# The meta tokens' products of 16 rows and 512 columns as two of 256 columns, from rows 0 and 32

## The chip, the cores and the metric

One core of a Trainium2 chip runs one program. The metric is the device time of one execution in microseconds (us). Names used throughout: PE is TensorE's matmuls, PEld its weight loads, DVE VectorE, ACT ScalarE, POOL GpSimd, SP the queue that issues the weight transfers, and PSUM the matmuls' output memory with banks of 512 float32 columns.

## The reference

Two blocks of a language model over 272 tokens: 16 learned meta tokens ahead of 256 real ones. The change is in the second block, which has two layers of this form (cut to what matters):

```
u = rmsnorm(h); proj = u @ w_in
pool_out = silu(pool_g) * pool_mixer(pool_v)
ssd_out  = ssd_mixer(...)        # chunks: 16 meta tokens, 128, 128
attn_out = silu(a_g) * attention # 8 heads, 2 kv heads, the same chunks as keys
h = h + rmsnorm(concat(pool_out, ssd_out, attn_out) @ w_out)

# ssd, per chunk and group of 8 heads
states = einsum('bcsgn,bcgrs,bcsgrp->bcgrpn', bm, decay_states, x * dt)
# attention, per kv head with its 4 query heads
o = einsum('bqgrk,bqkgd->bqgrd', softmax(logits), v)
```

The sum over the keys (k) and over a chunk's tokens (s) is the contraction of a matmul, so the meta tokens' part of it contracts over 16 rows only. Between the layers h has all 272 tokens; the second layer's output drops the meta tokens, so there the meta tokens serve only as keys and as the first state.

## The kernel before, in words

Activations lie with channels on the 128 partitions and tokens in columns. Nearly all of the work is `unit`: a projection's block of 128 output channels is summed over 16 (or 8) slices of 128 input channels, three matmuls a slice (`pj<-xh,whi`, `pj<-xl,whi`, `pj<-xh,wlo`), after ACT and DVE have split each 128x1024 piece of weights into a high (`whi`) and a low part (`wlo`). These are matmuls of type float32r over 256 to 272 columns.

What the heads need beside that runs as separate streams (Python generators) whose instructions are merged into the row of `pj` matmuls; their PSUM tiles are called `mx` (four buffers, `pst()`), and their matmuls are plain float32, which the trace shows as two passes each; a transpose (`tp`, L295, against the identity `c`) is one pass. A scheduler with a timing model of its own places every engine's instructions; each engine then runs its row strictly in order.

Three streams of the second block make the meta products. `attention` turns the values v around once per layer (`vT`, one tile for each of the three chunks of keys). `back_attention` handles each query chunk `ci` and kv head: probabilities `pr`, four transposes a key chunk into one PSUM tile, a copy to `pT`, then `po += vT.T @ pT` over the key chunks, 512 columns being 4 heads by 128 queries. `back_ssd` handles each group g of 8 heads: per chunk four transposes of x (`cx`) into `xd` and, times the decay, `xw`; one transpose of bm into `bt`; then the state `st = bt.T @ xw`, 128 by 512. In both, the meta chunk's product has operands of 16 rows. `back_dt` makes the transposed tables (`tdt`, `tdl`) with the decays per layer.

Of the kernel before, what the change touches and what calls it, by code (L numbers as in the profile page):

```python
# [17 lines left out]
P = 128  # L18
NM = 16
# [219 lines left out]
class Kernel:  # L239
# [53 lines left out]
    def tp(self, out, in_):  # L293
        n = in_.shape[0]
        return self.PE.transpose(out, in_, self.cst("ident")[:n, :n])  # L295

    def split(self, hi, lo, x):
        self.act(hi, x)
# [1250 lines left out]
    def back_dt(self, x):  # L1549
        reg, l, nc = self.early, self.l, self.nc  # L1550
        sm = lambda *shape, name, rows=P: self.p2.tile([rows, *shape], F32, tag="d_" + name, name=name, bufs=1)

        yield 6.0
        dt, cs, dl = (reg(T, rows=32, name=i) for i in ("dt", "cs", "dl"))
        base, tot = (reg(2, 8, rows=32, name=i) for i in ("base", "tot"))
        lp = self.log1pexp(x, 32, T, reg)
        self.stt(dt, x, 0.0, ALU.max, lp, ALU.add)
        da = x
        self.ts(da, dt, self.a, ALU.mult, -1.0, ALU.mult)
        self.V.tensor_tensor_scan(out=cs, data0=self.cst("sscan")[:32], data1=da, initial=0.0, op0=ALU.mult,  # L1560
                                  op1=ALU.add)
        cb = cs[:, NM:].rearrange("p (c b t) -> p c b t", c=2, b=8)
        self.V.tensor_copy(tot, cb[:, :, :, 15])
        self.V.memset(base[:, :, 0:1], 0.0)
        for c in range(2):
            self.V.tensor_tensor_scan(out=base[:, c, 1:], data0=self.cst("ones")[:32, :7], data1=tot[:, c, :7],
                                      initial=0.0, op0=ALU.mult, op1=ALU.add)
        for c in range(2):
            self.add(cb[:, c], cb[:, c], base[:, c].unsqueeze(2).to_broadcast([32, 8, 16]))
        self.dbg(f"L{l}cs", cs)  # L1570
        self.csd = self.dr.tile([32, T], F32, name=f"csd{l}")
        nc.gpsimd.dma_start(self.csd, cs)
        for o, m in ((0, NM), (NM, P)):
            self.ts(dl[:, o:o + m], cs[:, o:o + m], -1.0, ALU.mult, cs[:, o + m - 1:o + m], ALU.add)
        self.act(dl[:, :NM + P], dl[:, :NM + P], AF.Exp)

        self.tcs, self.tdt, self.tdl, self.tec = (sm(3, 32, name=f"t{i}") for i in range(4))
        yield 5.0
        pt = self.pst()
        p4 = pt[:, :288].rearrange("p (c x h) -> p c x h", c=3, x=3)  # L1580
        chunks = ((0, NM), (NM, P), (NM + P, P))
        for c, (o, m) in enumerate(chunks):
            for x_, src in enumerate((cs, dt, dl)):
                if c < 2 or x_ < 2:
                    self.tp(p4[:m, c, x_], src[:, o:o + m])
        for c, (o, m) in enumerate(chunks):
            self.act(self.tcs[:m, c], p4[:m, c, 0])
            self.act(self.tdt[:m, c], p4[:m, c, 1])
            self.act(self.tec[:m, c], p4[:m, c, 0], AF.Exp)
            if c < 2:  # L1590
                self.act(self.tdl[:m, c], p4[:m, c, 2])
        yield 1.0

    def rope(self, tmp, x, kind, o, n):
# [16 lines left out]
    def attention(self):  # L1611
        reg, l, o0, n = self.reg, self.l, self.o0, self.n
        all_ = slice(0, T)
        fl = lambda t: t.rearrange("p a b -> p (a b)")
        chunks = ((0, NM), (NM, P), (NM + P, P))
        qi = []
        for j in range(4):
            q = reg(2, n, name="qi")
            yield from self.unit(f"L{l}i_q{j}", self.xs, self.outc, lambda i, ps: self.nrm(q[:, i], ps, self.outc))
            self.rope(self.rt[j % 2][:, :, :n], q, "i", o0, n)  # L1620

            qs = [self.early(2, n, name="qs").bitcast(F32R) for _ in range(2)]
            for hh in range(2):
                r, o = slice(64 * hh, 64 * hh + 64), slice(64 - 64 * hh, 128 - 64 * hh)
                self.act(qs[hh][r], q[r])
                self.sub(qs[hh][o], q[r], qs[hh][r].bitcast(F32))
            qi.append(qs)
            if j == 0:

                self.tiw = self.p2.tile([P, 3, 32], F32, tag="d_tiw", name="tiw", bufs=1)  # L1630
                pt = self.pst()
                p3 = pt[:, :96].rearrange("p (c h) -> p c h", c=3)
                for c, (o, m) in enumerate(chunks):
                    if o + m > self.o0:
# [12 lines left out]
        qs, gs = [], []  # L1647
        for j in range(4):
            q = reg(2, n, name="q")
            yield from self.unit(f"L{l}a_q{j}", self.xs, self.outc, lambda i, ps: self.nrm(q[:, i], ps, self.outc))  # L1650
            self.rope(self.rt[j % 2][:, :, :n], q, "q", o0, n)
            qs.append(q)
            yield 1.0
            if j == 0:
                vT = []
                for o, m in chunks:
                    pt = self.pst()
                    for j in range(2):
                        self.tp(pt[:m, P * j:P * j + P], v[:, j, o:o + m])
# [48 lines left out]
    def back_attention(self, ng, k, vT, qs, gs):  # L1708
        reg, l, o0 = self.reg, self.l, self.o0
        chunks = ((0, NM), (NM, P), (NM + P, P))  # L1710
        sc = 128 ** -0.5
        for ci, (o, m) in enumerate(chunks):
# [3 lines left out]
            for kv in range(2):  # L1716
# [16 lines left out]
                pT = []  # L1733
                for si, (so, sn) in keys:
                    yield 1.0
                    pt = self.pst()
                    for i in range(4):
                        self.tp(pt[:sn, m * i:m * i + m], pr[i // 2][:, i % 2, so:so + sn])
                    t = reg(4 * m, rows=sn, name="pT")
# [6 lines left out]
                po = self.pst()  # L1746
                for x, (si, _) in enumerate(keys):
                    self.mm(po[:, :4 * m], vT[si][:, kv], pT[x], start=x == 0, stop=x == len(keys) - 1)
                for i in range(2):
                    self.stt(self.mix[:, 24 + 4 * kv + 2 * i:26 + 4 * kv + 2 * i, o - o0:o - o0 + m],  # L1750
                             po[:, 2 * m * i:2 * m * i + 2 * m].rearrange("p (h t) -> p h t", h=2), 0.5, ALU.mult,
                             gs[2 * kv + i][:, :, o - o0:o - o0 + m], ALU.mult)

    def front_ssd(self, g):
# [25 lines left out]
    def back_ssd(self, g, bc, xs, zs):  # L1780
# [20 lines left out]
        xd, st = [], []  # L1801
        for c, (o, m) in enumerate(chunks):
            yield 1.0
            pt = self.pst()
# [4 lines left out]
            xd.append(t)  # L1809
            if c == 2:  # L1810
                break
            w = reg(512, rows=m, name="xw")
# [7 lines left out]
            pS = self.pst()  # L1820
            self.mm(pS, bt, w)
            s = reg(512, name="st")
            if c == 0:
                self.act(s, pS)
            else:
                ed = self.p2.tile([P, 8], F32, tag="ed", name="ed", bufs=2)
                nc.gpsimd.dma_start(ed, self.csd[hs, NM + P - 1:NM + P].rearrange("(o h) t -> o (h t)", o=1)
                                    .to_broadcast([P, 8]))
                self.act(ed, ed, AF.Exp)
                self.mul(h8(s, P), h8(st[0], P), ed.unsqueeze(2).to_broadcast([P, 8, 64]))  # L1830
                self.add(s, s, pS)
            st.append(s)
        Ls = None
        y = [reg(2, n, name="y") for _ in range(2)]
# [114 lines left out]
```

## Time and profile before

| | before |
|---|---|
| time, median of 3 runs | 2941.95 us (2938.15 to 2943.53) |
| profiled execution | 2941.08 us |
| its span, first to last instruction | 2939.3 us |
| PE busy | 2890.7 us, 98% |
| DVE / ACT / POOL busy | 68% / 49% / 6% |
| mean granted TensorE clock | 0.994 |

A busy share is the time in which an engine had at least one instruction in flight. A matmul's duration in the trace overlaps the next one's, so what a matmul costs is read from the distance between starts, not from its duration.

### The profile page before, as it was taken

What the parts mean: (1) busy time and instruction counts of PE and PEld (TensorE: products, weight loads), DVE (VectorE), ACT (ScalarE), POOL (GpSimd) and SP (SyncE); (2) the same over time, 40 slices, a digit from 0 to 9 for tenths busy, and PEclk for the clock granted to TensorE, in tenths of its full rate; (3) what the DMA queues carried; (4) which work ended last, traced back from release to release, by engine and by line L of the source; (5) the groups of instructions that cost most, each with busy time, mean ns of one, the idle gap of its engine ahead of it and who ended that gap; (6) DMA issues with size and microseconds to landing.
All of it is one profiled execution on the core that took longest, in us unless ns stands there. A gap on an engine that the chain in (4) does not pass through costs nothing.

```text
span 2939.3 us, 56854 instructions
## 1 busy us (share of the span) xinstructions
PE 2890.7 (98%) x23398; PEld 2790.3 (95%) x23398; DVE 2003.0 (68%) x3520; ACT 1429.4 (49%) x2051; POOL 169.8 (6%) x331
## 2 busy tenths in 40 slices
PE   8999999999999999999999999999989999999997
PEld 8999999989999999999999999999989999999997
DVE  7657668657565555668866877764579678887555
ACT  6445546445354444456434444444465444444453
POOL 1101001001000000002000010000021000000000
PEclk9999999999999999999999999999999999999999
DMA  6534435435446565666554455555555545556553
GB/s 225 161 113 136 145 103 148 129 117 163 136 134 187 186 186 184 185 199 211 162 180 144 136 164 161 174 179 173 177 167 162 188 143 154 184 172 187 175 185 122
DMA packets 135028, 480.42 MB, mean 163 GB/s; under 512 B 18056, under 2 KB 18576, under 8 KB 134768
## 3 DMA queue, kind: packets, MB, share of 16 engines
q1 hardware_dynamic: 122112, 441.80, 48.0%
q0 software_dynamic: 12224, 33.90, 4.3%
q8 instruction: 183, 3.00, 0.4%
q10 hardware_dynamic: 432, 1.09, 0.1%
q14 instruction: 77, 0.63, 0.1%
HBM read 468.40 MB, written 7.02 MB: 162 GB/s over the span
## 4 chain that ended last, share of the span: by engine, by line
PE 94%; DVE 3%; DMA 1%; ACT 1%; issue 1%; POOL 0%; DVEq 0%; ACTq 0%; POOLq 0%
PE pj L291 81%; PE mx L291 11%; PE mx L295 2%; DVE wlo L270 1%; DMA wraw<-in_w_dram 1%; ACT L267 0%; DVE out L270 0%; DVE h L270 0%; DMA LB<-ld 0%; ACT whi L267 0%; DVE xl L288 0%; DMA h<-in_xt_dram 0%; POOL db L270 0%; DMA ld<-Dc 0%; DVE yc L270 0%
## 5 line engine op out<-in xcount | busy, mean ns | idle before, releaser
L291 PE MATMUL pj<-xh,whi 128*128 128x272 f32 (+2 forms) x6080 | 1749.5, 288 | 17.6 <-ACT xh L267 14.8
L291 PE MATMUL pj<-xh,wlo 128*128 128x272 f32 (+2 forms) x6080 | 1745.0, 287 | 1.0 <-DVE wlo L270 1.0
L291 PE MATMUL pj<-xl,whi 128*128 128x272 f32 (+2 forms) x6080 | 1744.1, 287 | 1.0 <-DVE xl L288 1.0
L267 ACT ACTIVATE whi<-wraw 128x1024 fp32r<-128x1024 f32 x840 | 886.9, 1058 | 1204.3 <-PE pj L291 1021.8
L270 DVE TENSOR_TENSOR wlo<-wraw,whi 128x1024 fp32r<-128x1024 f32 x840 | 1024.4, 1221 | 572.4 <-ACT whi L267 569.9
L291 PEld LDWEIGHTS pj<-xh,whi 128*128 128x128 f32 x6080 | 1142.2, 188 | 34.1 <-ACT xh L267 15.2
L291 PEld LDWEIGHTS pj<-xh,wlo 128*128 128x128 f32 x6080 | 1147.0, 189 | 10.7 <-issue 6.1
L291 PEld LDWEIGHTS pj<-xl,whi 128*128 128x128 f32 x6080 | 1145.4, 188 | 9.9 <-issue 5.1
L291 PE MATMUL pj<-yh,whi 128*128 128x256 f32 x384 | 108.1, 282 | 0.0
L291 PE MATMUL pj<-yl,whi 128*128 128x256 f32 x384 | 108.0, 281 | 0.0
L291 PE MATMUL pj<-yh,wlo 128*128 128x256 f32 x384 | 107.8, 281 | 0.0
L267 ACT ACT_TABLE_LOAD x79 | 101.4, 1283 | 4.3 <-PEq L1938 1.7
L291 PE MATMUL pj<-ml,whi 128*128 128x256 f32 x256 | 73.2, 286 | 0.0
L291 PE MATMUL pj<-mh,whi 128*128 128x256 f32 x256 | 73.2, 286 | 0.0
L291 PE MATMUL pj<-mh,wlo 128*128 128x256 f32 x256 | 72.9, 285 | 0.0
L291 PEld LDWEIGHTS pj<-yh,wlo 128*128 128x128 f32 x384 | 72.4, 189 | 0.0
L291 PEld LDWEIGHTS pj<-yh,whi 128*128 128x128 f32 x384 | 72.4, 189 | 0.0
L291 PEld LDWEIGHTS pj<-yl,whi 128*128 128x128 f32 x384 | 72.3, 188 | 0.0
L288 DVE SCALAR_TENSOR_TENSOR cx<-ct,hcw,cx 128x271 f32<-128x271 f32 (+2 forms) x144 | 64.3, 493 | 0.0
L291 PEld LDWEIGHTS pj<-mh,whi 128*128 128x128 f32 x256 | 49.6, 194 | 0.0
L291 PEld LDWEIGHTS pj<-mh,wlo 128*128 128x128 f32 x256 | 49.5, 193 | 0.0
L291 PEld LDWEIGHTS pj<-ml,whi 128*128 128x128 f32 x256 | 49.5, 193 | 0.0
(493 smaller groups left out, 2576.2 us busy)
## 6 DMA issues: line engine op xcount, KB each, us to landing
wraw<-in_w_dram SPq DMA_DIRECT2D x838, 512.0 KB, 3.5
L<-csd POOLq DMA_DIRECT2D x32, 256.0 KB, 4.9
LB<-ld POOLq DMA_DIRECT2D x12, 480.0 KB, 8.8
h<-in_xt_dram POOLq DMA_DIRECT2D x8, 272.0 KB, 9.5
h<-hd POOLq DMA_DIRECT2D x8, 272.0 KB, 3.8
hd<-h POOLq DMA_DIRECT2D x8, 272.0 KB, 2.4
res<-in_xt_dram POOLq DMA_DIRECT2D x8, 256.0 KB, 4.4
hd<-acc POOLq DMA_DIRECT2D x8, 256.0 KB, 3.6
```

Source lines behind the costliest of these rows:

```text
L267: return self.S.activation(out, in_, func, **kw)
L270: return (eng or self.V).tensor_tensor(out=out, in0=a, in1=b, op=op)
L288: return self.V.scalar_tensor_tensor(out=out, in0=a, scalar=s, in1=b, op0=op0, op1=op1)
L291: return self.PE.matmul(out, lhsT, rhs, start=start, stop=stop)
L295: return self.PE.transpose(out, in_, self.cst("ident")[:n, :n])
```

## The change

The meta chunk's operands come to lie twice below each other: heads' first half on rows 0 to 15, second half on rows 32 to 47 of a 64-row tile. The product of 16 rows by 512 columns becomes two of 16 rows by 256 columns, one from rows 0, one from rows 32, each into a PSUM bank of its own. To bring data to rows 32 and up, the new helper `tp32` transposes 32 columns instead of 16 (16 meta tokens and the 16 after them, which are not used) for row 0, and does the same with a plain matmul against the identity for row 32.

```
+    def tp32(self, out, row, cols, in_):
+        n, o = in_.shape[0], out[row:row + 32, cols]
+        if row == 0:
+            return self.tp(o, in_)
+        return self.mm(o, in_, self.cst("ident")[:n, :n])
...
@@ back_dt
+        self.mul(wm[:, :32], dt[:, :32], dl[:, :32])
+        for x in range(2):
+            self.tp32(pt, 32 * x, slice(0, 32), wm[:, :32])
+        self.act(self.twm, pt[:64, :32])
...
@@ attention (vT of the meta chunk)
+                            for x in range(2):
+                                self.tp32(pt, 32 * x, slice(P * j, P * j + P), v[:, j, :32])
...
@@ back_attention
+                    if si == 0 and ci:
+                        for i in range(4):
+                            self.tp32(pt, 32 * (i // 2), slice(m * (i % 2), m * (i % 2) + m), pr[i // 2][:, i % 2, :32])
+                        t = reg(2 * m, rows=64, name="pT")
+                        self.V.tensor_copy(t, pt[:64, :2 * m])
...
-                for x, (si, _) in enumerate(keys):
-                    self.mm(po[:, :4 * m], vT[si][:, kv], pT[x], start=x == 0, stop=x == len(keys) - 1)
+                    pos = [self.pst()[:, :2 * m] for _ in range(2)]
+                    for x in range(1, len(keys)):
+                        for i in range(2):
+                            self.mm(pos[i], vT[x][:, kv], pT[x][:, 2 * m * i:2 * m * i + 2 * m], start=x == 1, stop=False)
+                    for i in range(2):
+                        r = slice(32 * i, 32 * i + NM)
+                        self.mm(pos[i], vT[0][r, kv], pT[0][r], start=False, stop=True)
...
@@ back_ssd (meta chunk)
+                for i in range(4):
+                    self.tp32(pt, 32 * (i // 2), slice(P * (i % 2), P * (i % 2) + P), xs[i // 2][:, i % 2, :32])
+                for x in range(2):
+                    r = slice(32 * x, 32 * x + NM)
+                    self.mul(h4(w[r]), h4(pt[r, :256]),
+                             self.twm[r, 8 * g + 4 * x:8 * g + 4 * x + 4].unsqueeze(2).to_broadcast([NM, 4, 64]))
+                for x in range(2):
+                    self.tp32(pt, 32 * x, slice(0, P), bc[:, 0, :32])
+                self.act(bt, pt[:64, :P])
+                pS = [self.pst() for _ in range(2)]
+                for x in range(2):
+                    r = slice(32 * x, 32 * x + NM)
+                    self.mm(pS[x][:, :256], bt[r], w[r])
+                for x in range(2):
+                    self.act(s[:, 256 * x:256 * x + 256], pS[x][:, :256])
+                if o < o0:
+                    xd.append(None)
+                    continue
```

The four transposes of 16 columns for `xd` stay in the first layer, where the meta tokens have outputs, and fall away in the second. The key chunks of 128 rows keep their columns, in two matmuls of 256 instead of one of 512. In the whole program 12 matmuls of 128 rows by 512 columns become 24 by 256, 16 of 16 rows by 512 become 32 by 256 (16 from rows 32), 76 transposes of 16 columns become 16 (those of `xd`) plus 44 of 32 columns, and 44 plain matmuls of 32 columns are new, besides one transpose and one matmul of 32 by 32 in each layer.

The scheduler places the new instructions. First PE's row in the first layer's attention, chunk 1, kv head 0 (`pr` are the probabilities, `c_66` the identity; L295 is a transpose, L291 a plain matmul; the size is the output's). Before:

```order
L291 MATMUL pj<-xl,whi 128x272
L295 MATMUL mx<-c_66,pr 16x128
L295 MATMUL mx<-c_66,pr 128x128
L295 MATMUL mx<-c_66,pr 16x128
L295 MATMUL mx<-c_66,pr 128x128
L295 MATMUL mx<-c_66,pr 16x128
L295 MATMUL mx<-c_66,pr 128x128
L295 MATMUL mx<-c_66,pr 16x128
L295 MATMUL mx<-c_66,pr 128x128
L291 MATMUL pj<-xh,wlo 128x272
```

And with the change:

```order
L291 MATMUL pj<-xl,whi 128x272
L295 MATMUL mx<-c_66,pr 32x128
L295 MATMUL mx<-c_66,pr 128x128
L295 MATMUL mx<-c_66,pr 32x128
L295 MATMUL mx<-c_66,pr 128x128
L291 MATMUL mx<-c_66,pr 32x128
L295 MATMUL mx<-c_66,pr 128x128
L291 MATMUL mx<-c_66,pr 32x128
L295 MATMUL mx<-c_66,pr 128x128
L291 MATMUL pj<-xh,wlo 128x272
```

The two plain matmuls to rows 32 stand singly between transposes of 128 columns.

Second, PE's row in the first layer's SSD, group 1, where x (`cx`) and bm (`cx` too) of the meta chunk are turned around. Before, the four transposes of x:

```order
L291 MATMUL pj<-xl,whi 128x272
L291 MATMUL pj<-xh,wlo 128x272
L295 MATMUL mx<-c_66,cx 16x128 x4
L291 MATMUL pj<-xh,whi 128x272
L291 MATMUL pj<-xl,whi 128x272
```

With the change, x and bm follow each other:

```order
L291 MATMUL pj<-xh,whi 128x272
L291 MATMUL mx<-z,c_66 128x272
L295 MATMUL mx<-c_66,cx 32x128 x2
L291 MATMUL mx<-c_66,cx 32x128 x2
L295 MATMUL mx<-c_66,cx 32x128
L291 MATMUL mx<-c_66,cx 32x128
L291 MATMUL pj<-xl,whi 128x272
```

Two of x's transposes became plain matmuls, and bm's one transpose became a transpose and a plain matmul.

Third, the same group's state product (`xw,bt`). Before:

```order
L291 MATMUL pj<-xl,whi 128x272
L291 MATMUL pj<-xh,wlo 128x272
L291 MATMUL pj<-xh,whi 128x272
L291 MATMUL mx<-xw,bt 128x512
L295 MATMUL mx<-c_66,cx 128x128 x4
L291 MATMUL pj<-xl,whi 128x272
```

With the change:

```order
L291 MATMUL pj<-xh,whi 128x272
L291 MATMUL mx<-xw,bt 128x256
L291 MATMUL pj<-xl,whi 128x272
L291 MATMUL pj<-xh,wlo 128x272
L291 MATMUL pj<-xh,whi 128x272
L291 MATMUL pj<-xl,whi 128x272
L291 MATMUL mx<-xw,bt 128x256
L295 MATMUL mx<-c_66,cx 16x128 x4
L295 MATMUL mx<-c_66,cx 128x128 x4
```

The two halves are four `pj` matmuls apart. So are they in groups 2 and 3 of the first layer (seven apart) and group 0 of the second (one apart); the other four pairs of the SSD, and all eight of the attention, stand next to each other.

## Rows read from the trace of the kernel before

**Rows 1.** The page: busy us, share of the span, instructions of each engine.
```profile
PE 2890.7 (98%) x23398; PEld 2790.3 (95%) x23398; DVE 2003.0 (68%) x3520; ACT 1429.4 (49%) x2051; POOL 169.8 (6%) x331
```

**Rows 2.** The page: chain that ended last, share of the span by engine.
```profile
PE 94%; DVE 3%; DMA 1%; ACT 1%; issue 1%; POOL 0%; DVEq 0%; ACTq 0%; POOLq 0%
```

**Rows 3.** Waits of PE, 1370 to 2939: us in total, times, longest; first and last.
```profile
PE pj L291 <- ACT xh L267: 6.2, 1, 6.2
...
PE pj L291 <- DVE v L270: 0.8, 1, 0.8
```

**Rows 4.** Waits of DVE, same stretch: the longest in total.
```profile
DVE wlo L270 <- ACT whi L267: 285.9, 270, 3.2
```

**Rows 5.** Groups by form, PE, same stretch: the two meta products, by passes.
```profile
L291 PE MATMUL mx<-xw,bt 16*128 16x512 f32 x16 | 9.0, 640 | 0.0
...
L291 PE MATMUL mx<-pT,vT 16*128 16x512 f32 x16 | 8.9, 633 | 0.0
```

**Rows 6.** Timeline of PE at a meta product: start us, us, instruction, passes.
```profile
1614.34 0.29 PE L291 MATMUL pj<-xh,wlo 128*128 128x272 f32 x1
1614.47 0.29 PE L291 MATMUL pj<-xh,whi 128*128 128x272 f32 x1
1614.68 1.12 PE L291 MATMUL mx<-xw,bt 16*128 16x512 f32 x2
1615.73 0.73 PE L291 MATMUL mx<-k,q 128*128 128x272 f32 x2
1616.30 0.60 PE L295 MATMUL mx<-c,cx 128*128 128x128 f32 x4
1616.65 0.37 PE L291 MATMUL pj<-xl,whi 128*128 128x272 f32 x1
```

**Rows 7.** Timeline of PE at a state product of 128 rows.
```profile
1627.49 1.02 PE L291 MATMUL mx<-xw,bt 128*128 128x512 f32 x2
1628.35 0.60 PE L295 MATMUL mx<-c,pr 128*128 128x128 f32 x4
```

**Rows 8.** Timeline, first block: four matmuls of 64 rows, from rows 0 and 64.
```profile
37.68 0.28 PE L291 MATMUL pj<-xh,wlo 128*128 128x258 f32 x1
37.89 1.19 PE L291 MATMUL mx<-wa,wup 64*128 64x272 f32 x8
39.01 0.39 PE L291 MATMUL pj<-xh,whi 128*128 128x258 f32 x1
```

**Rows 9.** Timeline, first block: one matmul of 16 rows, 256 columns.
```profile
605.99 0.69 PE L291 MATMUL mx<-Dm,vm 16*128 16x256 f32 x2
606.62 0.92 PE L291 MATMUL mx<-D,vT 128*128 128x256 f32 x4
```

**Rows 10.** Timeline: four transposes of 16 columns among full matmuls.
```profile
1607.00 0.60 PE L295 MATMUL mx<-c,cx 128*16 128x128 f32 x4
1607.43 0.62 PE L291 MATMUL mx<-k,q 128*128 128x272 f32 x2
```

**Rows 11.** Timeline, first block: plain matmuls of 32 output columns.
```profile
307.33 0.29 PE L291 MATMUL pj<-xh,whi 128*128 128x272 f32 x1
307.55 0.44 PE L291 MATMUL mx<-E 128*32 128x32 f32 x8
307.91 0.40 PE L291 MATMUL pj<-xl,whi 128*128 128x272 f32 x1
308.14 0.29 PE L291 MATMUL pj<-xh,wlo 128*128 128x272 f32 x1
```

**Rows 12.** Timeline, first block: plain matmuls of 64 output columns.
```profile
167.73 0.65 PE L291 MATMUL mx<-Rk,vT 128*64 128x128 f32 x4
168.31 0.39 PE L291 MATMUL pj<-xh,whi 128*128 128x272 f32 x1
```

**Rows 13.** Timeline: four transposes right behind a meta product.
```profile
1700.45 0.65 PE L295 MATMUL mx<-c,cx 128*128 128x128 f32 x4
1700.86 0.37 PE L291 MATMUL pj<-xl,whi 128*128 128x272 f32 x1
```

More of the change, by code (lines that the diff above doesn't have):

```diff
@@ L1577, in back_dt @@
         self.tcs, self.tdt, self.tdl, self.tec = (sm(3, 32, name=f"t{i}") for i in range(4))
+        self.twm = sm(32, rows=64, name="twm")
+        wm = reg(32, rows=32, name="wm")
         yield 5.0
         pt = self.pst()
+        self.mul(wm[:, :32], dt[:, :32], dl[:, :32])
         p4 = pt[:, :288].rearrange("p (c x h) -> p c x h", c=3, x=3)
@@ L1591, in back_dt @@
                 self.act(self.tdl[:m, c], p4[:m, c, 2])
+        pt = self.pst()
+        for x in range(2):
+            self.tp32(pt, 32 * x, slice(0, 32), wm[:, :32])
+        self.act(self.twm, pt[:64, :32])
         yield 1.0
@@ L1657, in attention @@
                     pt = self.pst()
+                    m = m if o else 64
                     for j in range(2):
-                        self.tp(pt[:m, P * j:P * j + P], v[:, j, o:o + m])
+                        if o:
+                            self.tp(pt[:m, P * j:P * j + P], v[:, j, o:o + m])
+                        else:
+                            for x in range(2):
+                                self.tp32(pt, 32 * x, slice(P * j, P * j + P), v[:, j, :32])
                     t = reg(2, P, rows=m, name="vT")
@@ L1736, in back_attention @@
                     pt = self.pst()
+                    if si == 0 and ci:
[3 more added lines that the diff above has]
+                        self.V.tensor_copy(t, pt[:64, :2 * m])
+                        pT.append(t)
+                        continue
                     for i in range(4):
@@ L1745, in back_attention @@
                 yield 1.0
-                po = self.pst()
-                for x, (si, _) in enumerate(keys):
-                    self.mm(po[:, :4 * m], vT[si][:, kv], pT[x], start=x == 0, stop=x == len(keys) - 1)
+                if ci == 0:
+                    po = self.pst()
+                    self.mm(po[:, :4 * m], vT[0][:m, kv], pT[0])
+                    pos = [po[:, :2 * m], po[:, 2 * m:4 * m]]
+                else:
+                    pos = [self.pst()[:, :2 * m] for _ in range(2)]
[5 more added lines that the diff above has]
+                        self.mm(pos[i], vT[0][r, kv], pT[0][r], start=False, stop=True)
                 for i in range(2):
                     self.stt(self.mix[:, 24 + 4 * kv + 2 * i:26 + 4 * kv + 2 * i, o - o0:o - o0 + m],
-                             po[:, 2 * m * i:2 * m * i + 2 * m].rearrange("p (h t) -> p h t", h=2), 0.5, ALU.mult,
+                             pos[i].rearrange("p (h t) -> p h t", h=2), 0.5, ALU.mult,
                              gs[2 * kv + i][:, :, o - o0:o - o0 + m], ALU.mult)
@@ L1803, in back_ssd @@
             yield 1.0
+            if c == 0:
+                pt = self.pst()
+                for i in range(4):
+                    self.tp32(pt, 32 * (i // 2), slice(P * (i % 2), P * (i % 2) + P), xs[i // 2][:, i % 2, :32])
+                w = reg(256, rows=64, name="xw")
+                h4 = lambda t: t.rearrange("p (h v) -> p h v", h=4)
+                for x in range(2):
+                    r = slice(32 * x, 32 * x + NM)
+                    self.mul(h4(w[r]), h4(pt[r, :256]),
+                             self.twm[r, 8 * g + 4 * x:8 * g + 4 * x + 4].unsqueeze(2).to_broadcast([NM, 4, 64]))
+                yield 1.0
+                pt = self.pst()
+                for x in range(2):
+                    self.tp32(pt, 32 * x, slice(0, P), bc[:, 0, :32])
+                bt = reg(P, rows=64, name="bt")
+                self.act(bt, pt[:64, :P])
+                yield 1.0
+                pS = [self.pst() for _ in range(2)]
+                for x in range(2):
+                    r = slice(32 * x, 32 * x + NM)
+                    self.mm(pS[x][:, :256], bt[r], w[r])
+                s = reg(512, name="st")
+                for x in range(2):
+                    self.act(s[:, 256 * x:256 * x + 256], pS[x][:, :256])
+                st.append(s)
+                if o < o0:
+                    xd.append(None)
+                    continue
+                yield 1.0
             pt = self.pst()
@@ L1809, in back_ssd @@
             xd.append(t)
+            if c == 0:
+                continue
             if c == 2:
@@ L1822, in back_ssd @@
             s = reg(512, name="st")
[L1823 to L1831, printed above, removed]
+            ed = self.p2.tile([P, 8], F32, tag="ed", name="ed", bufs=2)
+            nc.gpsimd.dma_start(ed, self.csd[hs, NM + P - 1:NM + P].rearrange("(o h) t -> o (h t)", o=1)
+                                .to_broadcast([P, 8]))
+            self.act(ed, ed, AF.Exp)
+            self.mul(h8(s, P), h8(st[0], P), ed.unsqueeze(2).to_broadcast([P, 8, 64]))
+            self.add(s, s, pS)
             st.append(s)
```

## The prediction

> **What bounds the kernel now.** I read the page first: PE has something in flight for 98% of the span [rows 1], and the chain that ended last runs over PE for 94% [rows 2]. Busy is a weak measure, since matmuls overlap, so I went on to who waits for whom. In the stretch in which the second block runs (1370 to 2939 us) PE waits in six rows, from 6.2 down to 0.8 us, 12.4 us together [rows 3], and by the timeline these lie where one layer ends and the next begins. DVE on the other hand waits 285.9 us there for ACT's high parts of the weights alone [rows 4]. So PE's row of instructions is the clock of this kernel: what the change adds to that row is added to the time, and what it takes from DVE or ACT is worth nothing. The starts in the timeline then give the price of each kind of instruction. The usual pace of `pj` is 0.13 us from start to start (1614.34 to 1614.47 [rows 6]).
>
> **The meta products.** There are 16 passes of each of the two [rows 5], two passes a product, so 8 in the SSD and 8 in the attention. One takes 1.05 us from its start to the next instruction's (1614.68 to 1615.73 [rows 6]). The same 512 columns with 128 rows take 0.86 (1627.49 to 1628.35 [rows 7]). The reader is to see where the 0.19 comes from: a matmul that uses a part of the array's rows keeps neither its second pass nor its successor fed at once. Besides, the `pj` ahead lasts 0.21 instead of 0.13 us, and the k,q behind, two passes of 272 columns, 0.57 instead of 2 x 0.23 (272 columns at 0.86 us / 1024, or 0.84 ns a column). Going into a partial array and out of it so costs some 0.09 us ahead and 0.1 behind, in addition to the 0.19.
>
> Do two matmuls on different rows overlap? Four of 64 rows by 272 columns, alternately from rows 0 and 64, eight passes, took 1.12 us (37.89 to 39.01 [rows 8]); one after another they would be 8 x 0.23 = 1.83. So they run in pairs. A pair of 256 columns should take half of 0.86 and the same 0.19: 0.62, which saves 0.43 us a product. Entry and exit stay.
>
> In the rows of the changed order 12 of the 16 pairs stand together: 12 x 0.43 = **5.2 us saved**. Four halves of the SSD stand one to seven `pj` apart, and then each is a visit of its own: a lone matmul of 16 rows by 256 columns took 0.63 us (605.99 to 606.62 [rows 9]), two make 1.26, and one more entry and exit 0.19, together 1.45 against 1.05: 4 x 0.4 = 1.6, and 0.2 more in the second layer's group 0, where before the state product stood directly beside an attention product and shared its entry: **1.8 us lost**.
>
> Splitting 12 products of 128 rows into two of 256 columns leaves the columns as they are; their weights load under the pass before, as they do at 512. Nothing, or 0.1 us.
>
> **The transposes.** A transpose of 16 columns, 128 long, costs 0.43 / 4 = 0.11 us (1607.00 to 1607.43 [rows 10]) and fits in between full matmuls without entry or exit: its neighbours keep their pace. 60 stand where 76 stood: 16 x 0.11 = **1.7 us saved**. A transpose of 32 columns is not in the trace; a load of twice the columns under a pass of 0.11 us should stay hidden, so I take the price of 16.
>
> The 44 plain matmuls that bring data to rows 32 are the new cost. They have two passes where a transpose has one. Four passes of 64 output columns, 128 long, took 0.58 us (167.73 to 168.31 [rows 12]) of which, by 0.84 ns a column, 4 x 0.11 are the passes. 44 x 2 x 0.11 = **9.6 us lost**.
>
> And they use 32 of the array's columns. Rows 11 show what that costs: the `pj` ahead of eight such passes lasts 0.22 (307.33 to 307.55), the eight passes of 32 columns 0.36 instead of 8 x 0.027, and the first `pj` behind 0.23 (307.91 to 308.14) [rows 11]. That is 0.09 + 0.14 + 0.10 = 0.33 us for one run of partial columns, however long it is. Where a transpose follows instead of `pj`, the last part is smaller: four transposes behind a partial matmul took 0.41 (1700.45 to 1700.86 [rows 13]) against 0.35 behind a full one (1616.30 to 1616.65 [rows 6]), so 0.06; the run is then 0.29. In the changed order I count the runs, unbroken rows of such matmuls: 15 for `pr` (in seven of the eight cases the two stand singly, as the first pair of orders shows), 7 for x, 8 for bm, 4 for `vT`: 34, of which a transpose follows 20 and something else 14. 20 x 0.29 + 14 x 0.33 = **10.4 us lost**. This is the value I take, since form and neighbours are those of rows 11. The bounds: nothing, if such a matmul behind a transpose of the same 32 columns needs no change of the array, or 0.33 for each of the 34, 11.2 us, if a transpose behind is held up as long as `pj` is; the 64-column matmul gives the same (0.58 - 0.44 = 0.14 beside its passes [rows 12]).
>
> The Trainium skill speaks of this: TensorEngine Tiling (Array Packing), section Key Properties, says that changing the tiling mode, not just the tile, drains TensorE. It gives no price for a drain; with no price for it the sum below would come to 5.2 us, by the rows it is 15.6. The trace agrees with the rule in direction: 0.09 to 0.10 us are lost at either side [rows 11].
>
> The two 32 by 32 pairs of `back_dt` are a partial array from the start: a run of 0.33 each and a few short passes, **0.7 us**.
>
> **Beside PE.** DVE copies `pT` with half the columns, ACT copies the state in two pieces; DVE's 285.9 us of waiting cover either [rows 4]. If that cover were gone, one late `wlo` would hold PE, at 0.8 us each as in rows 3. No transfer is added, and none is moved past another on SP's or POOL's queue.
>
> **The sum.** -5.2 + 1.8 - 1.7 + 9.6 + 10.4 + 0.7 = +15.6 us. On the profiled execution's 2941.08 us that is 2956.7; the median of the runs shown is 0.9 above it, so 2957.6. I predict 2957 us, 0.5% slower. 0.2%, or 6 us, is about what a measurement of this kernel can tell from no change.
>
> **Rivals.**
> *Transpose and plain matmul overlap.* They write different 32 columns of the array from the same rows. If the plain one neither changes the array nor waits for its neighbour, the 34 runs cost nothing, and the 44 transposes beside them (4.8 us) disappear under them: 15.6 - 10.4 - 4.8 = +0.4, 2942. It decides (less than 6 us lost) once 9.6 of these 15.2 us fall away, that is with nearly all runs free. For it: the row pairs overlap [rows 8]. Against it: the transposes of 16 columns ignore the neighbours' full width [rows 10], so they seem to run on the full array, and leaving it costs 0.09. Ten in 100. The Trainium skill's TensorE: Matmul & The Clock Gate, section Packing small matmuls, lets tiles of different column groups run concurrently, and would give this 2942 if it held for a transpose; no row here has a transpose beside a partial matmul in another column group.
> *The halves on rows 0 and 32 don't overlap.* Then a pair lasts about 2 x 0.63, 0.64 more than taken: 12 x 0.64 = 7.7, 2965. Against it rows 8; they are of 64 rows, in groups of 0 and 64. Nine in 100.
> *A new wait.* Each product takes two of the four `mx` buffers until DVE or ACT has read both; the next user of that ring then blocks PE and all `pj` behind it. At 0.5 us for each of 16 products 8 us, 2965. Against it: PE waits for such a thing at no place now [rows 3], and the scheduler places the next user. Seven in 100.
> *All pairs overlap, and the way to rows 32 is free:* 16 x 0.43 saved, 2935. Two in 100; everything in rows 11 and 12 speaks against it.
>
> **The numbers.** The sum as worked out has 72 in 100; its own range is 2952 (half of the runs free) to 2959 (every run 0.33, and the split products not quite free). To hold 8 in 10 the range goes up to the two dearer cases and down to the point where most runs are free: 2949 to 2965. Slower by over 0.2%: 72 + 9 + 7 = 88; within 0.2%: 10; faster: 2.
>
> **What the changed profile would show.** In the timeline a meta pair, four passes of 16x256, has 0.6 us to its successor; a lone `pr` matmul to rows 32 about 0.3 us and a slow `pj` or transpose ahead and behind; PE's waits stay near 12 us and PE's busy share at 98%. I am wrong if plain matmuls start within 0.01 us of a transpose, if the pairs' second starts half a microsecond late, or if PE waits for DVE or ACT at a product.

## The result and the profile after

The changed kernel takes 2958.26 us (median of 4 runs, 2955.53 to 2960.72), the kernel before, measured beside it, 2942.74 (4 runs). The ratio is 1.0056, 95% interval 1.0039 to 1.0073: 0.56% slower, 15.5 us (11.5 to 21.5 by the interval). 2957 was predicted, in a range of 2949 to 2965.

The page of the profiled execution (2956.9 us, span 2955.1), first part, answers to [rows 1]:

```profile
PE 2903.5 (98%) x23532; PEld 2799.3 (95%) x23532; DVE 2000.7 (68%) x3526; ACT 1430.3 (48%) x2061; POOL 170.0 (6%) x333
```

PE is busy 12.8 us longer, ACT and DVE as long as before. The waits of PE in the second block, 1370 to 2955 us, answer to [rows 3] (three of seven rows):

```profile
PE mx L291 <- DVE mix L288: 1.3, 1, 1.3
PE mx L295 <- ACT dl L267: 1.2, 1, 1.2
...
PE mx L295 <- DVE wm L270: 0.6, 1, 0.6
```

All seven together are 14.4 us against 12.4. Three are new: PE stands once for `mix` and, at the second layer's tables in `back_dt`, for `dl` and for the new `wm`. Two rows of before, 0.8 us each for `wlo` and `v`, are gone. The wait for `mix` is in the first layer, right behind an attention product (first PE, then DVE):

```profile
1641.19 0.21 PE L291 MATMUL mx<-cx 128*16 128x16 f32 x2 [1.26 <-DVE mix L288]
1640.72 0.75 DVE L288 SCALAR_TENSOR_TENSOR mix<-mx,g 128x256 f32<-128x256 f32 x2
```

The two instructions of DVE read the product's two `mx` buffers. The matmul that writes an `mx` tile next starts when the first of them is done.

The rest is read from the distances between starts in PE's timeline. Four places of the changed kernel: a pair standing together, two halves standing apart, `pr`, and x with bm (start, us, instruction, passes):

```profile
1615.58 0.70 PE L291 MATMUL mx<-xw,bt 16*128 16x256 f32 x4
1616.21 0.73 PE L291 MATMUL mx<-k,q 128*128 128x272 f32 x2
...
1707.15 0.28 PE L291 MATMUL pj<-xh,whi 128*128 128x272 f32 x1
1707.36 0.69 PE L291 MATMUL mx<-xw,bt 16*128 16x256 f32 x2
1707.98 0.39 PE L291 MATMUL pj<-xl,whi 128*128 128x272 f32 x1
1708.22 0.29 PE L291 MATMUL pj<-xh,wlo 128*128 128x272 f32 x1
...
1657.52 0.27 PE L295 MATMUL mx<-c,pr 128*32 128x128 f32 x1
1657.63 0.39 PE L291 MATMUL mx<-cx 128*128 128x128 f32 x2
1657.85 0.38 PE L295 MATMUL mx<-c,pr 128*32 128x128 f32 x2
1658.16 0.41 PE L291 MATMUL mx<-c,pr 128*32 128x128 f32 x2
1658.50 0.33 PE L295 MATMUL mx<-c,pr 128*128 128x128 f32 x1
1658.76 0.41 PE L291 MATMUL mx<-c,pr 128*32 128x128 f32 x2
...
1701.24 0.38 PE L295 MATMUL mx<-c,cx 128*32 128x128 f32 x2
1701.55 0.62 PE L291 MATMUL mx<-c,cx 128*32 128x128 f32 x4
1702.11 0.29 PE L295 MATMUL mx<-c,cx 128*32 128x128 f32 x1
1702.32 0.41 PE L291 MATMUL mx<-c,cx 128*32 128x128 f32 x2
1702.66 0.39 PE L291 MATMUL pj<-xl,whi 128*128 128x272 f32 x1
1702.89 0.29 PE L291 MATMUL pj<-xh,wlo 128*128 128x272 f32 x1
```

- A pair of four passes takes 0.63 us to its successor (1615.58 to 1616.21) where the product of 512 columns took 1.05 [rows 6], one lone half of two passes 0.62 (1707.36 to 1707.98): the second half of a pair is free. A lone half pays its own way in and out: the `pj` ahead lasts 0.21, the one behind 0.24 instead of 0.13.
- A transpose of 32 columns ahead of a full matmul takes 0.11 (1657.52 to 1657.63). Two of them ahead of a plain matmul take 0.31 (1701.24 to 1701.55): 2 x 0.11 and 0.09 for going over to it. The row at 1657.85 takes the same 0.31; it merges one transpose of 32 columns with one of 128. Two plain passes take 0.34 (1658.16 to 1658.50) and four 0.56 (1701.55 to 1702.11): 0.11 each and 0.12. The transpose of 128 columns between two runs takes 0.26 (1658.50 to 1658.76): 0.11, 0.09 for the next run's entry, and 0.06 behind the last. One of 32 columns in such a place takes 0.21 (1702.11 to 1702.32), so there next to nothing is lost behind the last run. A `pj` behind a run takes 0.23 (1702.66 to 1702.89), 0.10 more than usual.

So a run of plain matmuls costs 0.09 + 0.12 + 0.06 = 0.27 us beside its passes ahead of a transpose, and 0.31 ahead of a `pj`. All 34 runs keep to these prices in the trace, and all 12 pairs that stand together take 0.63.

How the two executions differ by stretches is seen from the tile `iw`, which is made at the start of each layer (the row of its transposes, with the first and the last start; before, then after):

```profile
L295 PE MATMUL mx<-c,iw x5: 192/222/242, 1370.5 to 2184.5; 32*128 32x32 f32 x4, 32*16 32x32 f32 x1
```

```profile
L295 PE MATMUL mx<-c,iw x5: 192/220/245, 1368.4 to 2193.2; 32*128 32x32 f32 x4, 32*16 32x32 f32 x1
```

The unchanged first block was 2.1 us shorter in the execution of after, the first layer 10.8 longer (814.0 to 824.8), the second 7.1 longer (754.8 to 761.9): 17.9 in the block that the change touches. The 2.1 are no work of the kernel: the first block has the same matmuls in the same order in all fourteen traces of this document, and lasts from 1366.5 to 1377.9 us in them. In before a stretch of it ran at half clock, which after did not:

```profile
1259.50:1266.30 6.80, 6.80 (x33) 6.80 (x34) 0.42 (x1) 2.50 (x4) 0.00 (x0) 0.50 0.23 78
```

The columns are the stretch, its length, the busy us of PE, PEld, DVE, ACT and POOL, PE's granted clock (0.50, the lower of its two levels, 1.2 GHz), DMA share and GB/s.

In the windows of after PE ran at that level for 3.4 us behind the two waits at the tables, where before has no such stretch:

```profile
2248.80:2252.20 3.40, 3.40 (x18) 3.40 (x18) 2.78 (x9) 1.47 (x6) 2.20 (x4) 0.50 0.44 131
```

In it a matmul of 256 columns stands 0.21 us from the next instead of 0.12, so 3.4 us there lose some 1.6.

### The profile page after: what moved, and what is told of

It is laid out like the page before. It is cut to its first block, busy times and chain, and to the rows that moved or that the text cites. A ratio compares the mean times of both kernels' runs of the same rounds, so it can differ in the third digit from the quotient of the medians.

```text
span 2955.1 us, 57142 instructions
## 1 busy us (share of the span) xinstructions
PE 2903.5 (98%) x23532; PEld 2799.3 (95%) x23532; DVE 2000.7 (68%) x3526; ACT 1430.3 (48%) x2061; POOL 170.0 (6%) x333
## 4 chain that ended last, share of the span: by engine, by line
PE 94%; DVE 3%; DMA 1%; ACT 1%; issue 1%; POOL 0%; DVEq 0%; ACTq 0%; POOLq 0%
PE pj L291 80%; PE mx L291 11%; PE mx L295 2%; DVE wlo L270 1%; DMA LB<-ld 1%; ACT L267 0%; POOL db L270 0%; DVE h L270 0%; DVE out L270 0%; DMA ld<-Dc 0%; ACT whi L267 0%; DVE xl L288 0%; DMA h<-in_xt_dram 0%; DMA ed<-csd 0%; DVE yt L270 0%
## 5 line engine op out<-in xcount | busy, mean ns | idle before, releaser
L291 PE MATMUL pj<-xh,whi 128*128 128x272 f32 (+2 forms) x6080 | 1747.0, 288 | 17.0 <-ACT xh L267 14.5
L291 PE MATMUL pj<-xh,wlo 128*128 128x272 f32 (+2 forms) x6080 | 1745.7, 287 | 2.0 <-DVE wlo L270 1.9
L291 PE MATMUL pj<-xl,whi 128*128 128x272 f32 (+2 forms) x6080 | 1744.2, 287 | 1.0 <-DVE xl L288 1.0
L291 PEld LDWEIGHTS pj<-xh,whi 128*128 128x128 f32 x6080 | 1142.1, 188 | 34.6 <-ACT xh L267 14.9
L291 PEld LDWEIGHTS pj<-xh,wlo 128*128 128x128 f32 x6080 | 1147.3, 189 | 11.6 <-issue 5.9
L291 PEld LDWEIGHTS pj<-xl,whi 128*128 128x128 f32 x6080 | 1145.6, 188 | 9.9 <-issue 5.1
L291 PE MATMUL pj<-yh,whi 128*128 128x256 f32 x384 | 108.1, 282 | 0.0
L291 PE MATMUL pj<-yl,whi 128*128 128x256 f32 x384 | 108.1, 281 | 0.0
L291 PE MATMUL pj<-yh,wlo 128*128 128x256 f32 x384 | 107.9, 281 | 0.0
L291 PEld LDWEIGHTS pj<-yh,whi 128*128 128x128 f32 x384 | 72.5, 189 | 0.0
L291 PEld LDWEIGHTS pj<-yh,wlo 128*128 128x128 f32 x384 | 72.5, 189 | 0.0
L291 PEld LDWEIGHTS pj<-yl,whi 128*128 128x128 f32 x384 | 72.3, 188 | 0.0
L291 PE MATMUL pj<-ml,whi 128*128 128x256 f32 x256 | 72.0, 282 | 0.0
L291 PE MATMUL pj<-mh,whi 128*128 128x256 f32 x256 | 71.8, 281 | 0.0
L291 PE MATMUL pj<-mh,wlo 128*128 128x256 f32 x256 | 71.7, 280 | 0.0
L288 DVE SCALAR_TENSOR_TENSOR cx<-ct,hcw,cx 128x271 f32<-128x271 f32 (+1 forms) x144 | 64.2, 493 | 4.8 <-ACT cx L267 4.7
L291 PEld LDWEIGHTS pj<-mh,wlo 128*128 128x128 f32 x256 | 48.3, 188 | 0.0
L291 PEld LDWEIGHTS pj<-ml,whi 128*128 128x128 f32 x256 | 48.2, 188 | 0.0
L291 PEld LDWEIGHTS pj<-mh,whi 128*128 128x128 f32 x256 | 48.1, 188 | 0.0
```

The lines of the kernel that those rows point to most:

```text
L288: return self.V.scalar_tensor_tensor(out=out, in0=a, scalar=s, in1=b, op0=op0, op1=op1)
L291: return self.PE.matmul(out, lhsT, rhs, start=start, stop=stop)
```

## The experiments

The theory was the sum: what the change adds to PE's row is added to the time, 44 plain matmuls and 34 changes of the array against 12 overlapped products. Rivals were those of the prediction, and, once it was known that the row alone would explain nearly all, that the row is not the whole bound. Ratios are to the kernel before, in the runs that stood beside each (medians 2941.4 to 2943.4 us).

**e_double: each plain matmul to rows 32 issued twice.** The second writes the same values again.

```
             return self.tp(o, in_)
+        self.mm(o, in_, self.cst("ident")[:n, :n])
         return self.mm(o, in_, self.cst("ident")[:n, :n])
```

> Each of the 46 plain matmuls to rows 32 is issued twice, the second over the first. Theory (their passes stand alone in TensorE's row, 0.11 us each): 44 x 2 x 0.11 = 9.6 us more than the change, less some 2.5 us because the scheduler's new order has about 7 runs of partial columns fewer: +7 us, 2965. Rival (passes run beside the transposes, only entry and exit cost): 0 to -2 us, 2956 to 2958.

2967.2 us, 1.0086 (1.0070 to 1.0101), 8.9 above the changed kernel, where the theory had 7 and the rival 0 to -2. The timeline of the place with x and bm:

```profile
1708.42 1.06 PE L291 MATMUL mx<-c,cx 128*32 128x128 f32 x8
1709.41 0.28 PE L295 MATMUL mx<-c,cx 128*32 128x128 f32 x1
```

The run is 0.99 us long where it was 0.56: four more passes, 0.43. They stand alone in PE's row, at 0.11 each. That was the term of 9.6.

**e_plain: the 46 transposes beside them made plain matmuls too.** All 32-column matmuls are then of one kind, and those for rows 0 and 32 alternate.

```
-        if row == 0:
-            return self.tp(o, in_)
         return self.mm(o, in_, self.cst("ident")[:n, :n])
...
-                        for i in range(4):
+                        for i in (0, 2, 1, 3):
```

> The transposes of 32 columns to row 0 become plain matmuls too, in turn with those to row 32: two column groups of the array in one mode. Theory (tiles of one mode overlap, only a transpose cannot share the array with a partial matmul): the pairs start 0.01 us apart, 44 transposes of 0.11 us vanish under them and a few entries move: about 3 us below the change, 2955. Rival (column groups do not overlap): 44 x 0.11 us and more on top of the change, 2963 or above.

2956.11 us, 1.0050 (1.0037 to 1.0064); the rival's 2963 is above the interval. It overlaps that of after, so the time alone doesn't say that it is faster, but the timeline tells the mechanism:

```profile
1697.41 0.85 PE L291 MATMUL mx<-c,cx 128*32 128x128 f32 x12
1698.19 0.39 PE L291 MATMUL pj<-xh,wlo 128*128 128x272 f32 x1
```

Twelve passes take 0.78 us, 6 x 0.11 and 0.12; one after another they would be 1.32 and more. So two plain matmuls that write different 32 columns do run side by side, and the same work, which took 1.42 us in after (1701.24 to 1702.66), is done in 0.78 with 12 passes in place of 9. What could not run side by side was a transpose beside a plain matmul. The Trainium skill, TensorE: Matmul & The Clock Gate, section Packing small matmuls, lets tiles of different column groups run concurrently; the runs agree for plain matmuls, and show that it does not hold between a transpose and a plain matmul.

**e_attn and e_ssd: one part of the change alone**, the attention's (`attention`, `back_attention`) or the SSD's with its table (`back_ssd`, `back_dt`); the other functions are those of before. The products, after on the minus side:

```
@@ e_attn, back_ssd
-                    self.mm(pS[x][:, :256], bt[r], w[r])
+            self.mm(pS, bt, w)
@@ e_ssd, back_attention
-                        self.mm(pos[i], vT[0][r, kv], pT[0][r], start=False, stop=True)
+                    self.mm(po[:, :4 * m], vT[si][:, kv], pT[x], start=x == 0, stop=x == len(keys) - 1)
```

> The change's attention part alone, SSD as before: 20 plain matmuls to rows 32 in 19 runs, 8 pairs together, 20 transposes of 32 columns for 36 of 16. Theory by the prediction's prices: 20 x 0.22 + 13 x 0.29 + 2 x 0.33 + 4 x 0.29 - 8 x 0.43 - 16 x 0.11 = +5 us, 2946 to 2948. Rival (a wait is the cause, at the SSD): no more than 2 us, 2943.

> The change's SSD part alone, attention as before: 24 plain matmuls to rows 32 in 16 runs, 5 pairs together and 3 apart, as many transposes as before. Theory by the prediction's prices: 24 x 0.22 + 16 x 0.32 - 5 x 0.43 + 3 x 0.4 + 0.7 = +10 us, 2951, perhaps 1 less as one more pair stands together than in the change. Rival (a wait is the cause, wherever): the two parts do not add up to the 15 to 16 us of the whole.

e_attn took 2946.14 us, 1.0012 (1.0003 to 1.0020), and e_ssd 2954.23, 1.0037 (1.0022 to 1.0051): 3.5 and 11.6 us, together 15.1, as the whole. The parts add, as work in one row does, though the intervals are wide (0.9 to 5.9 and 6.5 to 15.0 us) and the sum can't tell such work from waits that each part brings with it. Among e_ssd's waits of PE are those for `dl` and `wm` (1.2 and 0.6 us), in e_attn they are missing: the SSD part brought them.

**e_wide: the plain matmuls taken out.** DVE copies the 32 columns of both halves next to each other, and one transpose of 64 columns puts them on rows 0 and 32. The 44 plain matmuls and their runs are gone, all 16 pairs stand together: the gain side of the change without its cost on PE. Pairs of heads are chosen so that each copy takes two of them.

```
+    def tp64(self, out, in_):
...
+        t = self.reg(2, 32, rows=n, name="w64")
+        self.V.tensor_copy(t, in_)
+        return self.tp(out, t.rearrange("p a b -> p (a b)"))
...
-                for i in range(4):
-                    self.tp32(pt, 32 * (i // 2), slice(P * (i % 2), P * (i % 2) + P), xs[i // 2][:, i % 2, :32])
+                for j in range(2):
+                    self.tp64(pt[:64, P * j:P * j + P], xs[j][:, :, :32])
```

> The pairs on rows 0 and 32 stay; the plain matmuls to rows 32 go: VectorE first copies the columns for both row groups next to each other (64 columns), and one transpose brings them to rows 0 to 31 and 32 to 63. In the built order no plain matmul of 32 columns is left, 44 transposes of 64 columns and 16 of 16 stand where 76 of 16 stood, and all 16 pairs stand together. Theory (TensorE's row of instructions is the time; the loss is passes and entries of the plain matmuls): 16 x 0.43 and 16 x 0.11 us saved against the kernel before, so about 8 us below it, 2934 to 2937, and 23 us below the change. Rival (the loss comes from the new order of the scheduler, with waits for PSUM and VectorE, which this one has too, and 44 copies more on VectorE): within 6 us of the change, above 2950.

2959.11 us, 1.0059 (1.0046 to 1.0071): no faster than the change. The forecast fell by over 20 us; the time is in the rival's band. The row itself holds what it was to hold: two transposes of 64 columns among full ones take 0.22 us, and a pair 0.63:

```profile
1455.48 0.38 PE L295 MATMUL mx<-c,w 128*64 128x128 f32 x2
1455.70 0.38 PE L295 MATMUL mx<-c,v 128*128 128x128 f32 x2
...
1626.97 0.70 PE L291 MATMUL mx<-xw,bt 16*128 16x256 f32 x4
1627.60 0.50 PE L291 MATMUL mx<-k,q 128*128 128x272 f32 x1
```

So the loss is looked for in the waits of PE (two rows of the second block that before has not):

```profile
PE mx L291 <- DVE z L270: 10.0, 4, 3.4
PE mx L295 <- DVE cs L1572: 3.0, 1, 3.0
```

`mx<-z` is the sum of squares at a group's end. The scheduler put that matmul 24 to 26 `pj` behind the transposes of `yt` in three groups of the first layer (61 to 71 in before), while what DVE and ACT do between takes longer. The windows at one of these waits show what follows it:

```profile
1706.40:1709.80 3.40, 0.04 (x1) 0.04 (x1) 2.80 (x5) 3.32 (x4) 0.00 (x0) 1.00 0.67 164
1709.80:1713.20 3.40, 3.40 (x13) 3.17 (x14) 0.81 (x4) 2.10 (x3) 0.00 (x0) 0.50 0.38 145
```

PE stands for 3.4 us and runs the next 3.4 at half its clock.

**w_attn and w_mix: e_wide's way in the attention alone, and there with the SSD of the second layer.** `back_ssd0` is that of before; w_attn uses it in both layers.

```
@@ w_mix
-        return self.back_ssd(g, bc, xs, zs)
+        return (self.back_ssd0 if l == 0 else self.back_ssd)(g, bc, xs, zs)
```

> The wide transposes (columns copied next to each other by VectorE, one transpose of 64 columns) in the attention alone; the SSD is that of the kernel before. In the built order all eight attention pairs stand together, no plain matmul of 32 columns is left, and the SSD's last matmul (z with the ones) stands 61 to 83 pj matmuls behind the transposes of yt, as in the kernel before (61 to 82), where in e_wide it stood 24 to 26 behind at three of the places. Theory (the row of TensorE holds what the step's prices say, and e_wide lost it to the new waits at that matmul): 8 x 0.43 and 16 x 0.11 us saved, no new wait: 5 us below the kernel before, 2936 to 2937. Rival (wide transposes or the copies cost as much as they save): 2941 or above.

> As w_attn, with the SSD's pairs and wide transposes in the second layer only, where no output of the meta tokens is needed; 12 pairs, all together. One of the eight places of the matmul z has 48 pj matmuls behind yt, the others 61 to 82. Theory: 12 x 0.43 and 24 x 0.11 us saved in the row, less the entries of one more 32-row transpose and some 2 to 4 us for a wait and half clock at the one short place: 2935 to 2939. Rival as for w_attn: 2941 or above.

w_attn took 2943.22 us, 1.0000 (0.9992 to 1.0009), w_mix 2951.88, 1.0031 (1.0019 to 1.0044). Both expectations fell. w_attn has one long wait of PE, at the same matmul at which before has its 0.8 us for `v` (first before, then w_attn), and in the windows behind it the lower clock:

```profile
1922.10 0.36 PE L291 MATMUL pj<-xh,whi 128*128 128x272 f32 x1 [0.77 <-DVE v L270]
```

```profile
1922.13 0.57 PE L291 MATMUL pj<-xh,whi 128*128 128x272 f32 x1 [6.77 <-DVE v L270]
```

```profile
1919.80:1926.60 6.80, 4.47 (x20) 4.50 (x21) 6.76 (x17) 0.66 (x1) 0.35 (x1) 0.50 0.54 174
```

That one wait eats what the row saved. Counted from the start of the layer, PE comes to this matmul 2.0 us sooner than in before, and goes on 4.0 us later, since the copy of `v` comes later; the runs do not show why it does. In the second layer, which has no such wait, the saving is there: it lasts 752.2 us (2186.6 to 2938.8) against 754.8, the 2.6 of 4 pairs and 8 transposes. w_mix has the wait for `v` too, and the waits at the second layer's tables.

**e_late and e_late_dt: e_wide with its early matmuls asked for later.** One number in each place, the pause that the stream makes ahead of them.

```
@@ back_ssd, ahead of the sum of squares (both)
-        yield 1.5
+        yield 3.0
@@ back_dt, ahead of the tables (e_late_dt)
-        yield 5.0
+        yield 12.0
```

> e_wide with one number changed: the sum of squares of the SSD is asked for later, so that the matmul of ones by z stands 63 to 82 pj matmuls behind the transposes of yt in every group; in e_wide it stood 24 to 26 behind them in the first three groups and 48 in the fifth. Theory (e_wide lost its gain to these four early matmuls): their four waits, 10.0 us, and the three stretches at half clock behind them (3.4, 3.4 and 6.8 us, which cost half of themselves, 6.8) go away: 2959.1 - 16.8 = 2942 us. Rival (e_wide's loss lies elsewhere, in DVE's copies that lay the halves side by side, or in PE's own row): 2955 us or more, with the waits for z gone and others in their place.

> e_late and one more number: the transposes of the second layer's tables stand 128 to 150 pj matmuls later than in e_wide, 35 to 54 later than in the kernel before. Theory: the waits for cs and dl (3.0 and 1.3 us) and the stretch of 6.8 us at half clock behind them (half of it lost, 3.4) go away too: 2942 - 7.7 = 2934 to 2936 us, which is the gain of the row's own work that e_wide was made to show. Rival: the waits move to other places of the second layer, 2942 us or more.

2961.05 us, 1.0058 (1.0046 to 1.0070), and 2960.42, 1.0059 (1.0046 to 1.0071). The waits for `z`, and in e_late_dt those at the tables, are gone as intended, and the time has not moved: the early matmuls alone did not cost e_wide its gain, since with them moved other waits of the same size stand in their place. The waits of PE in the first layer's stretch, 1570 to 1950, are in e_late_dt:

```profile
PE pj L291 <- DVE ct L270: 7.1, 5, 2.5
PE pj L291 <- DVE zt L270: 4.4, 2, 2.3
PE pj L291 <- DVE v L270: 2.5, 1, 2.5
PE pj L291 <- ACT whi L267: 1.1, 1, 1.1
```

Before, this stretch has a single wait of 0.8 us [rows 3]. `ct`, `zt` and `v` are the copies that empty a `pj` bank, so a `pj` waits for its bank. DVE's timeline at one of them (PE stood from 1766.76 to 1768.94):

```profile
1766.73 0.48 DVE L288 SCALAR_TENSOR_TENSOR cx<-ct,hcw,cx 128x269 f32<-128x269 f32 x1
1767.14 1.11 DVE L288 SCALAR_TENSOR_TENSOR y<-cx,parT,mx 128x128 f32<-128x128 f32 x4
1768.17 0.28 DVE L270 TENSOR_TENSOR cb<-mx,c 128x128 f32<-128x128 f32 x1
1768.37 0.77 DVE L270 TENSOR_TENSOR zt<-pj,R 128x272 f32<-128x272 f32 x2
```

No row has an idle time in brackets: DVE's row is full, and `zt<-pj` is behind in it. Yet in 1570 to 1900 the same DVE waits elsewhere for ACT (39.3 us in before):

```profile
DVE wlo L270 <- ACT whi L267: 44.5, 37, 3.8
```

So an engine can wait 44.5 us in a stretch and be late in the same stretch; its waiting ahead of a `wlo` serves no copy that stands behind that `wlo` in its row.

**e_late_pool: e_late_dt with the 46 side-by-side copies moved from DVE to POOL.** It was the test whether DVE's load made it late.

```
-        self.V.tensor_copy(t, in_)
+        self.G.tensor_copy(t, in_)
```

> e_late_dt with its 46 copies that lay the halves side by side moved from DVE to POOL; PE's row keeps its paired products and wide transposes. In e_late_dt the waits of PE went from the SSD's sum to the evacuations of pj by DVE in the first layer (ct, zt, v: 15.8 us in ten waits). Theory (the copies, 46 at 0.19 us, make DVE's row late where it had no slack): the ten waits shrink below 5 us and the stretches at half clock behind them go, 2960.4 - 11 - 5 = 2940 to 2946 us. Rival (DVE's load is not the cause, the order is: DVE's row asks for these evacuations too late whatever else it holds): the waits stay, 2953 us or more.

2945.44 us, 1.0005 (0.9996 to 1.0013): 15 us come back. (The waits that the expectation calls ten are nine, one of them, 1.8 us, in the second layer.) The waits of PE in 1570 to 1950 are now 5.2 us instead of 15.1:

```profile
PE pj L291 <- DVE zt L270: 2.8, 1, 2.8
PE pj L291 <- DVE v L270: 1.2, 1, 1.2
PE pj L291 <- DVE ct L270: 1.2, 1, 1.2
```

A copy on POOL takes longer, as the groups of POOL show (24 of the 46; behind the first bar busy us and the mean in ns; DVE took 199 ns for one in e_late_dt):

```profile
L306 POOL COPY w<-cx 128x64 f32<-128x64 f32 x24 | 17.8, 764 | 236.7 <-DVE cx L288 170.9 <-PE mx L291 65.8
```

POOL has the time, and these copies stand ahead of nothing there that PE needs. The Trainium skill, Perfetto Trace Analysis, section Optimizing Scalar/DVE Operations, says that moving work between GPSIMD and DVE might not help, as they share a read port; here the version with the copies on POOL is 15 us faster. The scheduler also placed other instructions anew (`mx<-z` of the first layer's four groups stands 68 to 81 `pj` behind the transposes of `yt`, where it stood 63 to 71 behind), so that load alone did it is argued, not shown. The saving of PE's row, some 8 us by e_wide's expectation, does not reach the time: PE's waits in the second block are still 19.0 us against 12.4, two of them for `rl` in the second layer (3.5 us), and two stretches of it, 6.8 and 3.4 us, run at the lower clock.

**w_l1 and w_l1_both: the paired products with wide transposes in the second layer alone**, in the attention, and there with the SSD; the first layer's rows are those of before (`attention0` is its function). w_l1_both also has the two pauses of e_late_dt in the second layer.

```
-        backs = yield from self.attention()
+        backs = yield from (self.attention0() if l == 0 else self.attention())
```

> The kernel before with the wide transposes and the paired products in the second layer's attention alone; the rows of the first layer are those of before. In w_attn the second layer was 2.6 us shorter than before, and all its loss was in the first. Theory: 4 pairs at 0.43 and 8 transposes at 0.11 are saved, 2.6 us, and no new wait: 2938.8 us against 2941.4. Rival (the gain goes to a new wait here too): 2941 us or more.

> w_l1 with the SSD's products of the second layer paired as well, with the wide transposes, the second layer's tables later as in e_late_dt, and its sums of squares later as in e_late. The first layer is that of before. Theory: beside the 2.6 us of w_l1, 4 pairs at 0.43 and 8 transposes at 0.11 are saved, 2.6 more: 2943.4 - 5.2 = 2938 us, if no wait comes with it. Rival (a wait of PE for v, as the 1.8 us with 3.4 us at half clock in e_late_dt's second layer, takes 3.5 of it): 2941.5 us or more.

w_l1 took 2940.30 us, 0.9990 (0.9980 to 0.9999), w_l1_both 2940.71, 0.9992 (0.9983 to 1.0001). The first is 3.1 us faster by the medians where 2.6 were expected, its interval just below 1, but that is less than the 0.2% that I called measurable; in its trace the second layer is only 1.3 us shorter than in before (753.5 us), with a new wait of 0.7 us for `rl`. The second, between its theory and its rival, adds nothing, with a new wait for `v` of 1.8 us in the second layer, as the rival had it. No version beats the kernel before by more than 0.1%.

## Why the prediction was right

- **PE's row is the clock.** Right for this change: its parts add to the whole (e_attn, e_ssd), and passes added to the row are added to the time (e_double). As a general sentence, "what it takes from DVE or ACT is worth nothing", it is half of the truth: moving 46 copies of 0.19 us from DVE to POOL, with the new order that came with it, was worth 15 us (e_late_dt against e_late_pool). The sign stood in before already: the prediction puts all waits of PE where layers meet, but the 0.8 us for `v` [rows 3] lie in the middle of a layer (1922.10), for a `pj` bank that DVE copies late.
- **Pairs together, 5.2 saved.** 0.63 us a pair where 0.62 was taken: 12 x 0.42 = 5.0. The rival in which the halves don't overlap would show 1.25 here.
- **Pairs apart, 1.8 lost.** A half 0.62, with entry and exit: as taken.
- **Transposes, 1.7 saved.** One of 32 columns costs the 0.11 of one of 16, as taken.
- **44 plain matmuls, 9.6 lost.** 0.11 a pass, alone in the row: as taken.
- **34 runs, 10.4 lost.** 0.27 and 0.31 where 0.29 and 0.33 were taken: 20 x 0.27 + 14 x 0.31 = 9.7. Reading their price from rows of another stage with the same form and neighbours [rows 11] was good to 7%.
- **`back_dt`, 0.7 lost.** The run itself is of that size; what was not seen is that PE now waits at the tables, 1.8 us, and runs 3.4 us at half clock behind it. With `mix` and the two that are gone the new waits are 2.0 us net of [rows 3], the clock 1.6: 3.6 that the sum did not have.

By the rows the sum is -5.0 + 1.8 - 1.7 + 9.6 + 9.7 + 0.7 + 3.6 = 18.7 against 17.9 measured in the second block; the first block, 2.1 shorter in this execution, brings the whole to 15.8. That 2957 came so near is in part luck: 3.6 us of waits and clock that were missing stand against 0.5 too much in the steps, 0.8 that the sum leaves open, and 2.1 of the first block, which no edit touched. Nor can the time confirm the sum to better than some 5 us, the half width of its interval; the steps rest on the timeline.

Of the rivals, *transpose and plain matmul overlap* is false as put, though two plain matmuls do it (e_plain). *A new wait* took place as this rival describes it, but small: at one of the 16 products PE stands 1.26 us until DVE has read a buffer of the pair (1641.19), where the rival had 0.5 us at each. That is one of the prediction's own signs of being wrong; the other 1.8 us stand at the tables, which it did not name. The cover named for DVE's and ACT's edits held but for that one place, but the argument for it, a total of 285.9 us [rows 4], was not sufficient: in e_late_dt the same row is 44.5 us in a fifth of that stretch, and PE waits 14 us for DVE there nevertheless.

## What to carry to other kernels

Matmuls on other rows of the array, or on other columns of it, do run side by side, but getting operands there may cost more than that saves: count the changes between full and partial array in the final order, at some 0.3 us each beside the passes. Where a small part of the array must be used, keep such matmuls of one kind and in one run; a transpose between them, even of 32 columns, went here at the pace of full matmuls and cost a change to the plain ones. An in-order engine's total waiting is no measure of the room in it: ask at the place whether the copy that frees a bank is ahead of PE or behind, before giving that engine 0.2 us of work 46 times.

## What was not expected of the hardware

A wait of PE can cost more than itself: behind the one of 3.39 us in e_wide the granted clock was 0.50 for 3.4 us, behind the one of 6.8 us in w_attn for 6.8 us, and behind 1.2 and 0.6 us close to each other in after for 3.4. A lone wait of 1.2 us in e_late_pool (at 1784) has no such stretch behind it, and the stretch at 1259.5 in before has no wait of PE ahead of it in the 19 us before: so the lower clock follows some waits and not others, and comes without one too. A transpose of 32 columns and a plain matmul that writes the 32 columns beside it do not overlap, and going from one to the other costs (0.09 us into the plain one), while two plain ones overlap fully (12 passes in 0.78 us).
